# One hybrid encoder trunk: the order of a projection's outputs, weights and products

## The chip, the cores and the metric

The kernel runs on one core of a Trainium2 chip. The metric is the device time of one execution in microseconds; three runs of the kernel before took 2345.83, 2346.84 and 2350.24 us, so its median is 2346.84. TensorE is called PE in the profile's rows, VectorE DVE, ScalarE ACT, GpSimd POOL, and SP is the engine whose queue issues most loads and stores.

## The reference

Two layers over 1024 time steps of width 1024, all in float32. What matters here are the two wide projections of each layer and what is done with each of their columns:

```python
for l in range(DEPTH):                       # 2 layers
    h = rmsnorm(x, norm1_w[l])
    q, k, v, g, z, xbc, dt_raw, lru_gate, lru_x = split_proj(h @ w_in[l])
    y_ret = retention(q, k, v, g)            # rotary on q and k
    y_ssd = ssd(z, xbc, dt_raw, ...)         # causal conv of width 4 and SiLU on xbc
    y_lru = rglru(lru_gate, lru_x, ...)      # causal conv of width 4 on lru_x, GeLU on lru_gate
    x = x + concatenate([y_ret, y_ssd, y_lru]) @ w_out[l]
    h = rmsnorm(x, norm2_w[l])
    u, v = causal_dwconv(h @ w_up[l])        # width 3, 2 x 2816 columns
    x = x + (gelu(u) * v) @ w_down[l]
return rmsnorm(x, final_norm_w)
```

## The kernel before

Activations lie with the 1024 channels on partitions, in 8 tiles of 128 x 512 for each half of the time (XA the first half, XB the second). A float32 product is made from a high and a low part of both operands: high x high, high x low, low x high (`PASSES`), so one block product over four channel tiles, called a product here, is 12 matmuls of 128x128 by 128x512 (`mm3`, `prod`). The parts are made by ScalarE (a copy that rounds, L205 and L236) and VectorE (the difference, L206 and L243); for weights GpSimd may take the difference by an accumulating DMA (L241).

A projection works through pairs of 128-column blocks: 12 pairs in an input projection, 22 in a feed-forward one. A pair is a 2 x 2 x 2 block problem (two column blocks, two halves of the channels, two halves of the time) done with seven products instead of eight, in the Strassen-Winograd way. `start` makes two of them from the first time half (operands `b11`, `b21`): the first result is u, copied from its bank by ScalarE (L834), and c11, their sum on VectorE (L837). `end` makes five, with operands `t2`, `t3`, `t1`, `b22`, `t4` of both time halves, and adds them on VectorE to the four results (L874 to L890). Their five weights come from `prep`: four additions or subtractions of raw weights on VectorE (L710), and five splits. The first pair uses eight plain products instead, four in `lead` and four in `follow`, because the operands of the second half don't exist yet.

`take` is what is done with a finished result: in the feed-forward projection a convolution (ScalarE L315, VectorE L318), the GeLU (L931), the product of the two columns (L933) and a store (L934); in the input projection a convolution with a gate (`xbc`, `lru`), a gate (`silu2`, `gelu2`) or the rotary (`rotate`: loads, and three VectorE operations L382 to L384).

`products` sets the order. Its `rest(0)` to `rest(3)` make the second half's operands: the norm's sum and its rows, then the blocks: `t1` and `b22` in `rest(2)`, `t2`, `t3` and `t4` in `rest(3)` (`blocks_b`, on VectorE with ScalarE). In between stand the products that need only the first half: `lead` of the first pair (p0) and `start` of the second and third (p1, p2). Then p0's `follow`, p1's `end`, p2's `end`, and from the fourth pair on `start` and `end` in turn. In the first layer's input projection (`raw`) the first half isn't normalised before its products; `scaled` multiplies the results by the rows, and p0's, p1's and p2's takes come after `rest(2)`. In the other three projections a first result is taken as soon as it is made.

The program's order is a priority: a planner at build time places each instruction on its engine's queue when its operands and a free buffer are there, the earliest in the program first, and each engine then works its queue in that order. Buffers that play a part: eight split weights (`wsplit`), three raw weights (`wraw`), eight tiles `t` (c11, u3, c22, a convolution's output, the rotary's tables), five tiles `c` (u), four banks each of `pp` and `ps`. `flip` gives two of three weight differences to GpSimd from the fourth pair on.

## Time and profile before

| what | value |
|---|---|
| median of three runs | 2346.84 us (2345.83 to 2350.24) |
| the profiled execution | 2346.2 us, span 2344.4 |
| TensorE busy | 2174.7 us (93%), 10494 matmuls |
| VectorE busy | 1924.6 us (82%) |
| ScalarE busy | 1288.4 us (55%) |
| GpSimd busy | 302.6 us (13%) |
| mean granted TensorE clock | 0.970 |

In order of time the first layer's input projection takes about 17 to 334, its mixers to 420, the output projection to 519, the feed-forward projection 519 to 962, the down projection to 1181; the second layer's input projection 1181 to 1474, mixers to 1566, output projection to 1662, feed-forward 1662 to 2106, down projection and final norm to the end. Times in the text are us on this axis, the profiled execution's span. Rows by stage give each engine's busy time in a stretch; rows in order of time give an instruction's start and length, and in brackets how long its engine stood idle before and what ended that. A line of a helper (L236, L243, L710, L300) stands for all its callers, so the tiles' names tell which one it is: `up` is a bank of a projection, `ws` a split weight, `wr` a raw one, `s` the weight sum S2, `bl` the low part of an operand block, `fc` a feed-forward convolution, `dtc` and `dtt` the time steps of the state-space mixer. Matmul records are missing now and then.

### The profile page before, as it was taken

The page shows a single profiled execution, that of the slowest core. Times are in us where ns is not written, and L with a number is a line of the kernel's source. Part 1 is how long each engine was busy: PE and PEld are TensorE (multiplying, and loading weights), DVE is VectorE, ACT ScalarE, POOL GpSimd, SP SyncE. Part 2 cuts the span into 40 slices and gives each one's busy share as a digit, 9 for nine tenths or more (in the row PEclk, how much of TensorE's full clock was granted, in tenths as well). Part 3 has the DMA queues.
Part 4 walks back from the last instruction along what each step waited for, and adds up shares of the span by engine and source line. Part 5 has one row for each costly group of instructions (what it writes and reads, how often), then busy time and mean ns, then how long its engine had stood idle before and what let it go on. Part 6 is the DMA issues. An engine that isn't in the chain of part 4 may idle for free.

```text
span 2344.4 us, 31562 instructions
## 1 busy us (share of the span) xinstructions
PE 2174.7 (93%) x10494; PEld 1758.3 (75%) x10494; DVE 1924.6 (82%) x3763; ACT 1288.4 (55%) x2370; POOL 302.6 (13%) x335
## 2 busy tenths in 40 slices
PE   6699988997999999999978989899989999999997
PEld 4477767885788888878866767777668888887787
DVE  7987858779877788999798877696797788789987
ACT  5357637554566556444445674674556665654443
POOL 0012213000222222000001131210002222210000
PEclk9799999999999999999988999999989999999999
DMA  4365687561666666854334638846437666677522
GB/s 173 108 149 134 150 248 233 167 209 48 149 150 148 145 153 152 285 193 137 108 128 123 152 79 235 266 150 208 137 93 164 144 148 148 147 197 254 178 83 73
DMA packets 176147, 371.94 MB, mean 159 GB/s; under 512 B 19440, under 2 KB 31856, under 8 KB 175984
## 3 DMA queue, kind: packets, MB, share of 16 engines
q1 hardware_dynamic: 135760, 297.55, 38.6%
q0 software_dynamic: 37440, 68.17, 17.1%
q10 hardware_dynamic: 2784, 4.20, 0.5%
q8 instruction: 83, 1.36, 0.3%
q14 instruction: 80, 0.66, 0.1%
HBM read 228.22 MB, written 69.27 MB: 127 GB/s over the span
## 4 chain that ended last, share of the span: by engine, by line
PE 65%; DVE 15%; DMA 8%; issue 7%; ACT 3%; SPq 1%; POOL 1%; DVEq 0%; POOLq 0%; ACTq 0%
PE up L300 43%; PE op L300 6%; PE dy L995 5%; PE dx L995 5%; PE dx L1071 2%; DMA ws<-wr 2%; DVE ws L243 2%; DVE bl L206 1%; DVE xb L318 1%; DMA cumb<-cumscr 1%; DMA tb<-in_rope_dram 1%; DMA g<-g1scr 1%; DMA g<-g0scr 1%; DVE g L710 1%; DMA wr<-in_w_ct_dram 1%
## 5 line engine op out<-in xcount | busy, mean ns | idle before, releaser
L300 PE MATMUL up<-bh,ws 128*128 128x512 f32 x3840 | 1228.2, 400 | 76.4 <-ACT ws L236 50.5
L300 PEld LDWEIGHTS up<-bh,ws 128*128 128x128 f32 x3840 | 735.6, 192 | 249.7 <-ACT ws L236 54.0
L300 PE MATMUL up<-bl,ws 128*128 128x512 f32 x1920 | 761.1, 398 | 11.8 <-DVE bl L206 11.7
L236 ACT ACTIVATE ws<-wr 128x512 fp32r<-128x512 f32 x568 | 348.7, 626 | 358.9 <-PE up L300 129.0
L300 PEld LDWEIGHTS up<-bl,ws 128*128 128x128 f32 x1920 | 369.2, 192 | 102.3 <-DVE bl L206 22.4
L241 POOL DMA_DIRECT2D ws<-wr x222 | 197.6, 905 | 1321.5 <-ACT ws L240 1046.0
L243 DVE TENSOR_TENSOR ws<-wr,ws 128x512 fp32r<-128x512 f32 x346 | 236.5, 688 | 61.0 <-ACT ws L236 54.9
L995 PE MATMUL dy<-ws,ws 128*128 128x512 f32 x792 | 192.2, 390 | 3.2 <-ACT ws L236 1.6
L995 PE MATMUL dx<-ws,ws 128*128 128x512 f32 x792 | 190.8, 390 | 2.1 <-ACT ws L236 1.2
L995 PEld LDWEIGHTS dy<-ws,ws 128*128 128x128 f32 x792 | 148.2, 188 | 36.4 <-DVE ws L243 3.3
L995 PEld LDWEIGHTS dx<-ws,ws 128*128 128x128 f32 x792 | 148.4, 188 | 34.1 <-ACT ws L236 2.1
L318 DVE SCALAR_TENSOR_TENSOR fc<-u,smalls,fc 128x512 f32<-128x512 f32 (+2 forms) x176 | 131.0, 748 | 50.6 <-ACT fc L315 49.6
L240 ACT ACTIVATE ws<-ws 128x512 fp32r<-128x512 f32 x260 | 159.8, 626 | 4.6
L300 PE MATMUL op<-yh,ws 128*128 128x512 f32 x512 | 160.5, 394 | 0.2 <-ACT yh L213 0.2
L318 DVE SCALAR_TENSOR_TENSOR fc<-c,smalls,fc 128x512 f32<-128x512 f32 (+2 forms) x176 | 131.2, 745 | 0.7 <-ACT fc L315 0.3
L315 ACT ACTIVATE fc<-c,smalls 128x512 f32<-128x512 f32 x88 | 71.2, 809 | 103.7 <-DVE c L837 101.7
L243 DVE TENSOR_TENSOR ws<-g,ws 128x512 fp32r<-128x512 f32 (+1 forms) x165 | 103.1, 649 | 13.7 <-ACT ws L236 13.5
L236 ACT ACTIVATE ws<-g 128x512 fp32r<-128x512 f32 (+1 forms) x165 | 92.1, 590 | 39.7 <-PE dy L995 13.8
L300 PEld LDWEIGHTS op<-yh,ws 128*128 128x128 f32 x512 | 95.4, 188 | 21.7 <-ACT yh L213 2.1
L300 PE MATMUL op<-yl,ws 128*128 128x512 f32 x256 | 100.3, 394 | 0.0
L710 DVE TENSOR_TENSOR wr<-wr,wr 128x512 f32<-128x512 f32 x64 | 44.9, 702 | 63.0 <-DMA wr<-in_w_up_dram 28.3
L236 ACT ACTIVATE ws<-s 128x512 fp32r<-128x512 f32 x64 | 40.4, 632 | 101.3 <-DVE s L710 92.4
(303 smaller groups left out, 2939.3 us busy)
## 6 DMA issues: line engine op xcount, KB each, us to landing
ws<-wr POOLq DMA_DIRECT2D x222, 256.0 KB, 4.3
wr<-in_w_up_dram SPq DMA_DIRECT2D x96, 512.0 KB, 4.3
wr<-in_w_dn_dram SPq DMA_DIRECT2D x66, 512.0 KB, 3.9
wr<-in_w_ct_dram SPq DMA_DIRECT2D x56, 512.0 KB, 4.7
wr<-in_w_o_dram SPq DMA_DIRECT2D x32, 512.0 KB, 5.1
g0scr<-fc SPq DMA_DIRECT2D x44, 256.0 KB, 3.3
g<-g0scr SPq DMA_DIRECT2D x44, 256.0 KB, 5.8
g1scr<-fc SPq DMA_DIRECT2D x44, 256.0 KB, 2.9
```

Source lines behind the costliest of these rows:

```text
L206: eng.tensor_tensor(lo, src, hi.bitcast(F32), op=ALU.subtract)
L236: act.activation(w[:, 0, :m], raw, AF.Copy)
L240: act.activation(w[:, 1, :m], w[:, 0, :m].bitcast(F32), AF.Copy, scale=-1.0)
L241: pool.dma_start(w[:, 1, :m].bitcast(F32), raw, accum_op=ALU.add)
L243: eng.tensor_tensor(w[:, 1, :m], raw, w[:, 0, :m].bitcast(F32), op=ALU.subtract)
L300: pe.matmul(dst, W(k, a), A(k, b), start=first and i == 0, stop=last and i == n - 1)
L315: act.activation(dst, body(x), AF.Identity, bias=bias, scale=taps(n))
L318: dve.scalar_tensor_tensor(dst[:, o:HT], x[:, HALO - j + o : HALO - j + HT], taps(n - j), dst[:, o:HT], op0=ALU.mult, op1=ALU.add)
L710: eng.tensor_tensor(o, a, b, op=op)
L995: pe.matmul(d[oc], w[:, a, P * oc : P * oc + P], t[:, b], start=not more and i == 0 and k == 0, stop=i == NP - 1 and k == 2, skip_group_ch ...
L1071: pe.matmul(X[oc][:, e], w[x][:, P * oc : P * oc + P], t[:, y, e], start=False, stop=i == NP - 1 and k == 2, skip_group_check=True)
```

## The change

Three things are changed, for all four projections.

- The order in `products`. p0's `lead` and the two `start`s no longer take their results. After `rest(2)` come `scaled`, p0's `follow` without its takes, the `prep` of p1, `rest(3)`, and only then the takes of p0, first half (`firsts`) and second half (`followed`). p1's `prep`, which stood at the head of its `end`, thus goes in front of `rest(3)`, and each later pair's first results are taken just before its `end`. The first layer's case and the others now have one order; `lead` and `ahead` are fixed at 1 and 2.
- The order in `end`. The product of `t1` comes first, into a bank z; ScalarE copies z into c22, and the product of `b22` is accumulated into the same bank after that (`more` leaves out the start flag). One addition of u with z stands for two, and c22 is completed with u3 from memory. The order of products is t1, t2, b22, t3, t4 instead of t2, t3, t1, b22, t4.
- The order of the splits in `prep`: w1, w2, w4, w3, w22 instead of w2, w3, w1, w4, w22.

```diff
@@ -291,13 +291,13 @@
             return x
         return get
 
-    def mm3(dst, W, A, ks, first=True, last=True):
+    def mm3(dst, W, A, ks, first=True, last=True, more=False):
 
         n = 3 * len(ks)
         i = 0
         for k in ks:
             for a, b in PASSES:
-                pe.matmul(dst, W(k, a), A(k, b), start=first and i == 0, stop=last and i == n - 1)
+                pe.matmul(dst, W(k, a), A(k, b), start=first and i == 0, stop=last and i == n - 1, skip_group_check=more)
                 i += 1
 
 
@@ -781,8 +781,8 @@
         sp.dma_start(r[:, : 2 * HT], src)
         return r[:, :HT], r[:, HT : 2 * HT]
 
-    def prod(d, w, B, name, first=True, last=True):
-        mm3(d, lambda k, a: w[:, a, P * k : P * k + P], lambda k, b: B[name, k][b], range(4), first, last)
+    def prod(d, w, B, name, first=True, last=True, more=False):
+        mm3(d, lambda k, a: w[:, a, P * k : P * k + P], lambda k, b: B[name, k][b], range(4), first and not more, last, more)
 
     class Pair:
 
@@ -790,7 +790,7 @@
         def __init__(self, src, B, take):
             self.src, self.B, self.take, self.ready, self.w, self.q = src, B, take, None, None, None
 
-        def lead(self, raw):
+        def lead(self):
 
             B = self.B
             self.v = []
@@ -808,8 +808,6 @@
                 c = halo(t_tile, "c11")
                 dve.tensor_add(body(c), body(u), d2)
                 self.v.append((c, u))
-                if not raw:
-                    self.take(m, 0, c, u)
 
         def follow(self):
 
@@ -820,14 +818,14 @@
                 prod(d, w1, self.B, "t1", last=False)
                 prod(d, w2, self.B, "b22", first=False)
                 dve.tensor_add(body(u), body(u), d)
+
+        def followed(self):
+            for m, (_, u) in enumerate(self.v):
                 self.take(m, 1, u)
 
-        def start(self, reload=False, raw=False):
-            if self.ready:
-                w11, w12 = self.ready
-            else:
-                q = up_raw(self.src[0])
-                w11, w12 = part_of(q[0]), part_of(q[1])
+        def start(self, reload=False):
+            q = up_raw(self.src[0])
+            w11, w12 = part_of(q[0]), part_of(q[1])
             d1, d2 = p_bank("up"), s_bank("up")
             prod(d1, w11, self.B, "b11")
             self.u = halo(c_tile, "u")
@@ -837,15 +835,17 @@
             dve.tensor_add(body(c11), body(self.u), d2)
             self.q = None if reload else q
             self.v = [(c11, self.u)]
-            if not (reload and raw):
-                self.scaled()
 
         def scaled(self):
 
-            for m, (c, u) in enumerate(self.v):
-                if "raw" in self.B:
+            if "raw" in self.B:
+                for c, u in self.v:
                     dve.tensor_tensor(body(c), body(c), self.B["raw"], op=ALU.mult)
                     dve.tensor_tensor(body(u), body(u), self.B["raw"], op=ALU.mult)
+
+        def firsts(self):
+
+            for m, (c, u) in enumerate(self.v):
                 self.take(m, 0, c, u)
 
         def prep(self):
@@ -856,11 +856,10 @@
             s3 = a11
             s2 = tp.tile([P, HT], F32, tag="xl", name=nm("s2"), bufs=2)
             sub(dve, s2, a22, s3)
-            w2, w3 = part_of(s2), part_of(s3)
             sub(dve, a21, a21, a22, ALU.add)
-            w1 = part_of(a21)
+            w1, w2 = part_of(a21), part_of(s2)
             sub(dve, a12, a12, s2)
-            w4, w22 = part_of(a12), part_of(a22)
+            w4, w3, w22 = part_of(a12), part_of(s3), part_of(a22)
             self.w = w1, w2, w3, w4, w22
 
         def end(self):
@@ -869,21 +868,21 @@
                 self.prep()
             w1, w2, w3, w4, w22 = self.w
             u = body(U)
-            d = p_bank("up")
+            U3, C22 = halo(t_tile, "u3"), halo(t_tile, "c22")
+            u3, c22 = body(U3), body(C22)
+
+            z = p_bank("up")
+            prod(z, w1, B, "t1")
+            act.activation(c22, z, AF.Copy)
+            d = s_bank("up")
             prod(d, w2, B, "t2")
             dve.tensor_add(u, u, d)
+            prod(z, w4, B, "b22", more=True)
             d = s_bank("up")
             prod(d, w3, B, "t3")
-            U3, C22 = halo(t_tile, "u3"), halo(t_tile, "c22")
-            u3 = body(U3)
             dve.tensor_add(u3, u, d)
-            d = p_bank("up")
-            prod(d, w1, B, "t1")
-            dve.tensor_add(u, u, d)
-            dve.tensor_add(body(C22), u3, d)
-            d = s_bank("up")
-            prod(d, w4, B, "b22")
-            dve.tensor_add(u, u, d)
+            dve.tensor_add(u, u, z)
+            dve.tensor_add(c22, c22, u3)
             self.take(0, 1, U)
             d = p_bank("up")
             prod(d, w22, B, "t4")
@@ -891,30 +890,29 @@
             self.take(1, 0, U3, C22)
             self.take(1, 1, C22)
 
-
-    def products(pairs, rest, later, lead, ahead, raw=False):
-
-        n = lead + ahead
-        for j, p in enumerate(pairs[:n]):
-            if j < lead:
-                p.lead(raw)
-            else:
-                p.start(True, raw)
-            if j < n - 1:
-                rest(j)
-        rest(2)
-        for j, p in enumerate(pairs):
-            by_dma[0] = j >= n
-            if j >= n:
+    def products(pairs, rest, later, ahead=2):
+
+        p = pairs[0]
+        p.lead()
+        rest(0)
+        for j in range(1, ahead + 1):
+            pairs[j].start(True)
+            rest(j)
+        p.scaled()
+        p.follow()
+        pairs[1].prep()
+        rest(3)
+        p.firsts()
+        p.followed()
+        for f in later.get(0, ()):
+            f()
+        for j, p in enumerate(pairs[1:], 1):
+            by_dma[0] = j > ahead
+            if j > ahead:
                 p.start()
-            elif raw:
-                p.scaled()
-            if j == 1:
-                rest(3)
-            if j < lead:
-                p.follow()
-            else:
-                p.end()
+            p.scaled()
+            p.firsts()
+            p.end()
             for f in later.get(j, ()):
                 f()
         by_dma[0] = False
@@ -1233,7 +1231,7 @@
             rest = lead(B, XA, XB, first[0])
             pairs[0].ready = ready
         later = {0: [] if l else [setup], 1: [dt_a, dt_b], 3: [dt_c]}
-        products(pairs, rest, later, *((1, 2) if l else (1, 2)), not l)
+        products(pairs, rest, later)
         after = mixers(l, dts, skip(l))
         XA = out_proj(l, 0, y_split(l, 0, after), src)
         SB = y_split(l, 1, last_dma[0])
@@ -1250,7 +1248,7 @@
         XB = out_proj(l, 1, SB, src, hook)
         sB = squares(lambda k: XB[k], f=d_tile)
         spill(xs1, XB, 1)
-        products([ffn_pair(l, j, B) for j in range(NF)], rest_of(B, XA, XB, sB, w2), {}, *((1, 2) if l else (1, 2)))
+        products([ffn_pair(l, j, B) for j in range(NF)], rest_of(B, XA, XB, sB, w2), {})
         XA, XB, last, others = ffn_down(l, None)
         if l + 1 < DEPTH:
             B, st = {}, {}
```

## Rows read from the trace of the kernel before

**Rows 1.** Stages: us; busy PE, PEld, DVE, ACT, POOL; clock; DMA share; GB/s.

```profile
26.00:110.00 84.00, 57.44 (x213) 37.34 (x214) 80.60 (x176) 26.38 (x49) 0.00 (x0) 0.81 0.30 97
...
519.00:592.00 73.00, 58.44 (x231) 42.57 (x230) 64.60 (x121) 34.90 (x55) 0.00 (x0) 0.90 0.18 56
592.00:962.00 370.00, 370.00 (x1630) 306.28 (x1629) 298.08 (x498) 222.84 (x362) 75.94 (x88) 1.00 0.65 157
...
1181.00:1262.00 81.00, 59.11 (x246) 44.68 (x245) 74.36 (x136) 36.42 (x61) 0.86 (x1) 0.83 0.39 127
```

**Rows 2.** Waits in total: us, times, the longest; TensorE.

```profile
PE up L300 <- ACT ws L236: 50.5, 8, 17.1
```

**Rows 3.** Order of time, TensorE, 1221 to 1241: start, us, engine, line, operation, tiles [idle before].

```profile
1240.40 0.80 PE L300 MATMUL up<-bh,ws 128*128 128x512 f32 x1 [17.09 <-ACT ws L236]
```

**Rows 4.** Order of time, VectorE, 1236 to 1241.

```profile
1237.20 0.68 DVE L206 TENSOR_TENSOR bl<-xd,bh 128x512 fp32r<-128x512 f32 x1
1237.80 0.68 DVE L710 TENSOR_TENSOR wr<-wr,wr 128x512 f32<-128x512 f32 x1
...
1240.81 0.68 DVE L206 TENSOR_TENSOR bl<-xd,bh 128x512 fp32r<-128x512 f32 x1
```

**Rows 5.** Order of time, TensorE, 580 to 589.

```profile
587.94 0.79 PE L300 MATMUL up<-bh,ws 128*128 128x512 f32 x1 [5.42 <-ACT ws L236]
```

**Rows 6.** Order of time, VectorE, 582 to 588.

```profile
583.16 0.68 DVE L710 TENSOR_TENSOR wr<-wr,wr 128x512 f32<-128x512 f32 x1
583.76 2.73 DVE L318 SCALAR_TENSOR_TENSOR fc<-u,smalls,fc 128x512 f32<-128x512 f32 x4
...
586.48 0.68 DVE L710 TENSOR_TENSOR s<-wr,wr 128x512 f32<-128x512 f32 x1
```

**Rows 7.** Order of time, TensorE, 98 to 112.

```profile
109.28 0.60 PE L418 MATMUL dtt<-mats,dtc 16*128 16x16 f32 x4 [10.02 <-DVE dtc L413]
```

**Rows 8.** Order of time, VectorE, 111 to 113.

```profile
111.35 0.68 DVE L710 TENSOR_TENSOR wr<-wr,wr 128x512 f32<-128x512 f32 x1
```

**Rows 9.** Groups of VectorE, 1201.7 to 1209.2, then 1218.8 to 1240.3: count, busy, mean ns.

```profile
L318 DVE SCALAR_TENSOR_TENSOR xb<-c,smalls,xb 128x511 f32<-128x511 f32 (+2 forms) x3 | 2.2, 748 | 0.0
...
L382 DVE TENSOR_TENSOR u<-u,tb 128x512 f32<-128x512 f32 x2 | 1.4, 680 | 0.0
```

**Rows 10.** Order of time, TensorE, 1256 to 1266.

```profile
1256.71 0.40 PE L403 MATMUL dt<-bh,wds 128*16 128x512 f32 x1
...
1260.43 0.40 PE L300 MATMUL up<-bh,ws 128*128 128x512 f32 x1
...
1265.67 0.40 PE L403 MATMUL dt<-bh,wds 128*16 128x512 f32 x1
```

**Rows 11.** Order of time, load queue, 532 to 596.

```profile
575.19 1.55 SPq L781 DMA_DIRECT2D wr<-in_w_up_dram  x2
...
595.07 2.64 SPq L781 DMA_DIRECT2D wr<-in_w_up_dram  x2
```

**Rows 12.** Groups of the whole run.

```profile
L882 DVE TENSOR_TENSOR u<-u,up 128x512 f32<-128x512 f32 x64 | 43.7, 683 | 19.9 <-PE up L300 19.3
...
L834 ACT ACTIVATE u<-up 128x512 f32<-128x512 f32 x64 | 37.5, 586 | 19.7 <-PE up L300 19.7
```

**Rows 13.** Order of time within one pair: ScalarE, then VectorE.

```profile
684.08 0.57 ACT L834 ACTIVATE u<-up 128x512 f32<-128x512 f32 x1
...
688.28 0.82 ACT L315 ACTIVATE fc<-c,smalls 128x512 f32<-128x512 f32 x1 [3.11 <-DVE c L837]
...
687.57 0.68 DVE L837 TENSOR_TENSOR c<-u,up 128x512 f32<-128x512 f32 x1
...
692.25 0.74 DVE L318 SCALAR_TENSOR_TENSOR fc<-c,smalls,fc 128x510 f32<-128x510 f32 x1
...
697.26 0.69 DVE L886 TENSOR_TENSOR u<-u,up 128x512 f32<-128x512 f32 x1 [0.67 <-PE up L300]
```

**Rows 14.** Waits in total, ScalarE on VectorE.

```profile
ACT fc L315 <- DVE c L837: 101.7, 37, 4.1
```


## The prediction

> **What bounds the kernel now.** I read the busy time by stage first, then who waits for whom on TensorE, then the order of time around its longest stalls.
>
> By stage [rows 1], TensorE is busy for all 370 us of the middle of the first feed-forward projection: 1630 recorded matmuls, 370 / 1630 = 0.227 us each, so a product of 12 takes 2.72 us and a pair of 84 takes 19.1 us. VectorE is at 298 of 370 there. Nothing taken off VectorE or ScalarE can shorten that stretch. The starts of the four projections are different: in 26 to 110, 519 to 592 and 1181 to 1262 VectorE works 81 of 84, 65 of 73 and 74 of 81 us, TensorE 57 to 59, and its granted clock averages 0.81 to 0.90; the second feed-forward start, 1662 to 1735, repeats the first. These 311 us are bound by VectorE, which makes the second half's operands, the weight sums and the finished outputs in one queue.
>
> Among TensorE's waits [rows 2] one for a split weight lasted 17.1 us. In time it lies at 1223 to 1240, in the second layer's input projection [rows 3]. All that p1 (the second pair) then needs is weights, but its first subtraction `wr<-wr,wr` starts only at 1237.80, among the last block splits [rows 4]. In the feed-forward starts the 5.42 us at 582.5 to 587.9 [rows 5] wait for p2 (the third pair): its subtractions stand at 583.16 and 586.48, with four convolution operations of p1's outputs between [rows 6]. In the first input projection the 10.02 us end at 109.28 [rows 7], with p2's subtractions at 111.35 [rows 8].
>
> **The change, part by part.** VectorE's operations start 0.60 us apart when it is saturated [rows 4]; I count with that, and 0.66 for a convolution's.
>
> (a) *First results behind the blocks.* In the second layer's input projection 8 operations of outputs ran among the first blocks (1201.7 to 1209.2: three convolution, three rotary, two gate, of which the first kind is shown), 8 x 0.62 = 5.0 us, and 6 rotary ones, 3.6 us, among the last [rows 9]. All 14 go behind the last block.
>
> (b) *p1's weights ahead of them.* Three of its four subtractions already stood before the last block; one subtraction and five splits, 6 x 0.60 = 3.6 us, are new in front. The last block then ends at 1241.5 - 5.0 - 3.6 + 3.6 = 1236.5 (1241.5 is 1240.81 + 0.68 in [rows 4]), and p1's last product 2.7 us later, at 1239, where now it ends at 1256.7 [rows 10]. The stall of 17 us goes.
>
> What is late next is p2: its weight sums stand behind everything put off. 14 output operations (8.6 us), p1's 5 additions (3.0), p1's three own convolutions with gates (3 x (3 x 0.66 + 0.6), 7.7), then three subtractions (1.8): 1236.5 + 21.1 = 1257.6, and about 0.9 for the split. So p2 begins at 1258.5, against 1260.4 now [rows 10]: 1.9 us. The work is conserved; what is gained beside it is what TensorE can do in the wait: 16 time-step matmuls that now stand behind p2's start (16 x 0.23 = 3.7 [rows 10]) and the two first products of p3 (24 x 0.227 = 5.4). Together 11.0; I take 9, because the two products need weights through the same load queue as the rotary tables. Bounds: 0 if VectorE's order keeps both out, 17.1 if p2's sums slip ahead of the outputs.
>
> In the feed-forward starts p1's weights are mostly made already. p2's start there is conserved less one addition (0.6). But its raw loads, now at 575.2, wait for p1's last two splits, and p3's come at 595 [rows 11]. With p1's splits ahead of the blocks both come before 575, and p3's two products (5.4) fit into the wait for p2: 6.0, of which I take 5, twice. Bounds for each: 3.0 us lost (five of p1's output operations, now after the subtraction, come before it because p1 ended sooner) to 8.4 gained (the 5.42 and 3 of slow restart). In the first input projection outputs stood behind two blocks' rounds already; the same sum gives 6.0, and I take 4, since `dtc` stays where it is in VectorE's queue. Bounds: 2 lost, 10.0 gained.
>
> More is issued past each queue: the loads of p1's weights go ahead of 24 rotary loads on the load queue, which shields them; the output stores come later, and nobody reads them in this stage. Tiles are the hidden cost: four first results are now held to the end of the blocks in a pool of eight, from which the rotation's three, and p1's two outputs, come too. A shortage delays outputs, not blocks.
>
> (c) *S1 T1 first, S4 B22 in its bank.* For 64 pairs VectorE loses one addition of six, the first on the bank of t1, 43.7 us in all; the other is kept, from memory instead of the bank. ScalarE gains a copy like the one of the first product, 37.5 us per 64 [rows 12]. In the middles both are hidden by TensorE's full queue [rows 1]: nothing. In the starts the addition is in the 0.6 above. The matmul count is unchanged. New is a wait: B22's product may not write the bank until ScalarE has copied it. Between stands t2's product, 2.72 us, against a copy of 0.59. The nearest row is the copy of a pair's first product: L886 begins at 697.26, released by its product, so the first product of that pair ended five products earlier, 697.2 - 13.6 = 683.6, and its copy began at 684.08 [rows 13]: 0.5 late, where 2.1 may be lost. I take nothing; the bounds are nothing and the second rival. If the cover goes, everything on TensorE behind that matmul waits, weight splits behind the copy on ScalarE too.
>
> Queue order, weighed: ScalarE's next convolution waited until 688.28, 3.11 us, for a VectorE sum [rows 13], and 37 such waits took 101.7 us, the longest 4.1 [rows 14]. The Trainium skill ("TensorE: Matmul & The Clock Gate", on engine queue depths) says that ScalarE takes its queue strictly in order, so that a copy behind such a wait waits too. By the row alone the sum keeps its zero; by that rule it would be the second rival's, and the trace agrees as far as order goes.
>
> **Sum.** 9 + 4 + 5 + 5 = 23 us off the profiled execution's 2346.2 (span 2344.4 and 1.8 around it) gives 2323.2; the median 2346.84 lies 0.64 above it, so 2324.
>
> **Rivals.** *The stalls only move* (0.18). VectorE's work ahead of p2 is conserved, and p3's weights don't arrive: four times 0.6 is left, 2344 to 2345. For it: VectorE is busy for 65 to 81 us of those stretches. Against it: TensorE had no filler because raw tiles came late, and these come sooner.
>
> *The copy holds up TensorE in the middles* (0.17, the slower one). If ScalarE's order puts the copy behind p's first GeLU, it waits for the sum L837, a convolution and two VectorE operations, the last of which starts at 692.25 and ends at 692.99, 6.6 us after the second product's end at 686.4; with GeLU (0.62) and copy (0.59) the bank is read at 7.8, where t1 and t2 allow 5.4. Each such pair costs 2.4 us; it decides from 1 pair in 5 on (10 of the 42 feed-forward pairs eat the 23 us). At 2 in 5, 17 x 2.4 = 41: 2365. For it: the waits of [rows 14] come once in nearly every pair. Against it: without the GeLU in front the copy ends 1.2 + 0.68 + 0.81 + 0.59 = 3.3 us after the second product, 2.1 us in time.
>
> *p2's sums slip ahead* (0.15). If held tiles stall the outputs, VectorE turns to p2 at once: 17.1 + 10.0 + 2 x 8.4 = 44 off, 2302.
>
> **Chances.** The forecast has 0.50, with its own range 2311 to 2337. From 2300 to 2358 about 8 in 10 is held: below is the tail of the last rival, above most of the slower one. A measurement can tell 0.2%, 4.7 us, from no change: faster is the forecast, the last rival and a quarter of the first (0.68), the same the rest of the first (0.15), slower the second rival (0.17).
>
> **What would show it.** Right: no TensorE wait of 17 us in the second input projection, with p1's first subtraction before its last round of blocks; p1's last product there ends near 1239 on this axis; a wait for p2's weights follows; p3's first products stand ahead of p2's others; the middles stay at 19.1 us a pair. Wrong: matmuls in the middles that wait for ScalarE's copy; p2's start unmoved with nothing new ahead of it; outputs in the stretch of the blocks as before.

## The result: 0.55% slower, and the profile after

The changed kernel took 2360.93 us (median of four runs, 2356.99 to 2363.38) against 2348.32 us of the kernel before on the same chip: a ratio of 1.0055, interval 1.0039 to 1.0071. The forecast, 23 us faster, was wrong in sign. The profiled execution took 2356.99 us with a span of 2355.2.

The part of the page with busy time:

```profile
PE 2180.1 (93%) x10494; PEld 1753.2 (74%) x10494; DVE 1896.9 (81%) x3699; ACT 1314.6 (56%) x2434; POOL 304.9 (13%) x335
```

VectorE has 64 operations less and ScalarE 64 more, as the change says. By stage, in the same columns and stretches, moved with each stage's start, as [rows 1]:

```profile
26.00:110.00 84.00, 63.41 (x234) 41.95 (x234) 79.53 (x173) 30.54 (x57) 1.00 (x1) 0.82 0.31 94
525.00:598.00 73.00, 62.07 (x249) 44.99 (x247) 65.47 (x122) 35.60 (x57) 0.00 (x0) 0.93 0.18 59
598.00:973.00 375.00, 371.63 (x1635) 306.87 (x1636) 284.95 (x476) 230.95 (x383) 75.94 (x88) 1.00 0.66 158
1188.00:1269.00 81.00, 68.09 (x283) 49.32 (x282) 79.37 (x145) 37.30 (x64) 0.86 (x1) 0.92 0.41 128
```

The starts look as forecast: 18 to 37 matmuls more in each, VectorE at least about as full as before (79.5 of 84, 65.5 of 73 and 79.4 of 81 us). New is the third line. The middle of the first feed-forward projection, where TensorE had no idle time before, now has 375.00 - 371.63 = 3.4 us of it. TensorE's waits in total (us, times, the longest) show what is new:

```profile
PE up L300 <- ACT ws L236: 43.4, 10, 8.1
PE up L300 <- ACT c L876: 16.7, 12, 3.2
...
PE dtt L418 <- DVE dtc L413: 7.5, 1, 7.5
PE dtt L418 <- DVE dtc L415: 6.9, 2, 6.6
```

Waits for split weights fell from 50.5 us [rows 2]; L876, the new copy of T1's bank, is a new group of 16.7; and the second layer's time-step transposes, which did not wait before, wait 6.6.

Order of time, TensorE, second layer's input projection, whose start is now at 1188.2 (1181.0 before):

```profile
1246.60 0.80 PE L300 MATMUL up<-bh,ws 128*128 128x512 f32 x1 [3.18 <-ACT ws L236]
...
1267.34 0.60 PE L418 MATMUL dtt<-mats,dtc 16*128 16x16 f32 x4 [6.57 <-DVE dtc L415]
```

The 17.09 us of [rows 3] are gone. The first line is already the first product of p2. VectorE's order in the same stretch shows why it is so early:

```profile
1221.26 0.70 DVE L710 TENSOR_TENSOR wr<-wr,s 128x512 f32<-128x512 f32 x1
...
1236.53 0.69 DVE L382 TENSOR_TENSOR c<-c,tb 128x512 f32<-128x512 f32 x1
...
1241.95 0.69 DVE L206 TENSOR_TENSOR bl<-xd,bh 128x512 fp32r<-128x512 f32 x1
...
1243.82 0.69 DVE L710 TENSOR_TENSOR wr<-wr,wr 128x512 f32<-128x512 f32 x1
...
1251.40 0.75 DVE L318 SCALAR_TENSOR_TENSOR xb<-c,smalls,xb 128x511 f32<-128x511 f32 x1
```

p1's last subtraction now stands at 1221.26, the last block's low part at 1241.95, and three operations behind it, at 1243.82, p2's first subtraction; most of the outputs that the forecast put in between (a convolution at 1251.40) come after. Not all 14 went behind the last block, either: six rotary operations (L382 to L384, the first at 1236.53) still run among the last low parts, as many as the forecast counted there before [rows 9]. The last block's low part still ends 54.4 us after the stage's start where it ended at 60.5, a little sooner than the forecast's 55.5.

The second group of waits, in one pair of the first feed-forward (p5): ScalarE's two lines, then TensorE's two:

```profile
658.15 0.81 ACT L315 ACTIVATE fc<-c,smalls 128x512 f32<-128x512 f32 x1 [5.21 <-DVE c L835]
658.88 0.58 ACT L876 ACTIVATE c<-up 128x512 f32<-128x512 f32 x1
...
657.25 0.39 PE L300 MATMUL up<-bh,ws 128*128 128x512 f32 x1
659.50 0.50 PE L300 MATMUL up<-bh,ws 128*128 128x512 f32 x1 [1.87 <-ACT c L876]
```

T2's last matmul begins at 657.25 and ends at 657.64, so T1's product ended 2.72 us before that, at 654.9. Its copy begins only at 658.88, 4.0 us later, because it stands behind a convolution that waited 5.21 us for a VectorE sum. T2's product covers 2.7 of 4.0 + 0.6; the rest, 1.9, is TensorE's idle time before B22. VectorE shows why that sum, L835, was late:

```profile
654.24 0.69 DVE L710 TENSOR_TENSOR wr<-wr,wr 128x512 f32<-128x512 f32 x1 [3.04 <-DMA wr<-in_w_up_dram]
...
657.44 0.68 DVE L835 TENSOR_TENSOR c<-u,up 128x512 f32<-128x512 f32 x1
```

It stands behind a subtraction that waited 3.04 us for its raw weights, and four more operations. So one late load is handed on through two queues before it reaches TensorE.

### The profile page after: what moved, and what is told of

Read it like the earlier page. It is cut to its first block, busy times and chain, and to the rows that moved or that the text cites. A ratio compares the mean times of both kernels' runs of the same rounds, so it can differ in the third digit from the quotient of the medians.

```text
span 2355.2 us, 31426 instructions
## 1 busy us (share of the span) xinstructions
PE 2180.1 (93%) x10494; PEld 1753.2 (74%) x10494; DVE 1896.9 (81%) x3699; ACT 1314.6 (56%) x2434; POOL 304.9 (13%) x335
## 5 line engine op out<-in xcount | busy, mean ns | idle before, releaser
L318 DVE SCALAR_TENSOR_TENSOR fc<-u,smalls,fc 128x512 f32<-128x512 f32 (+2 forms) x176 | 130.4, 749 | 12.3 <-ACT fc L315 11.8
L883 DVE TENSOR_TENSOR u<-u,up 128x512 f32<-128x512 f32 x64 | 43.9, 686 | 84.9 <-PE up L300 84.9
```

Of the source, the lines that this page charges most:

```text
L318: dve.scalar_tensor_tensor(dst[:, o:HT], x[:, HALO - j + o : HALO - j + HT], taps(n - j), dst[:, o:HT], op0=ALU.mult, op1=ALU.add)
L883: dve.tensor_add(u3, u, d)
```

## The experiments

All ratios are to the kernel before on the same chip, with 95% intervals. The stage lengths are read from one trace each: from a projection's first matmul to the next one's (the first from the span's start, the last to its end). For an input projection this takes in the mixers and the output projection, for a feed-forward one its down projection.

| kernel | ratio | input 1 | feed-forward 1 | input 2 | feed-forward 2 |
|---|---|---|---|---|---|
| before | 1 | 518.7 | 662.3 | 481.2 | 682.2 |
| changed | 1.0055 | 525.4 | 662.8 | 485.4 | 681.6 |
| e_order: (a), (b) alone | 1.0012 | 517.8 | 659.2 | 486.3 | 676.7 |
| e_end: (c) alone | 1.0156 | 523.4 | 668.9 | 498.7 | 686.4 |
| e_late: B22 behind T3 | 0.9962 | 519.7 | 659.1 | 481.0 | 677.5 |
| e_bank: B22's own bank | 1.0007 | 523.9 | 663.5 | 472.6 | 683.8 |
| e_split: before, split order | 1.0207 | 532.7 | 667.4 | 501.1 | 687.4 |
| e_endlate: (c) alone, B22 behind T3 | 1.0107 | 521.1 | 663.7 | 492.8 | 684.9 |
| e_hold: output projection held | 1.0062 | 526.2 | 663.3 | 490.1 | 682.8 |
| b_hold: before, held | 1.0008 | 518.0 | 661.4 | 479.6 | 678.9 |
| e_no_a | 1.0123 | 528.2 | 661.3 | 494.4 | 681.5 |
| e_no_b | 1.0091 | 522.7 | 663.0 | 490.3 | 683.8 |
| e_latesum | 1.0051 | 528.1 | 663.8 | 480.9 | 680.1 |
| e_last | 1.0005 | 519.3 | 658.2 | 490.1 | 676.8 |
| e_dvecopy | 1.0178 | 530.0 | 667.5 | 489.7 | 689.1 |
| e_ffn | 0.9982 | 517.7 | 660.4 | 479.1 | 677.6 |
| e_combo | 0.9948 | 513.0 | 659.5 | 474.3 | 678.5 |

How far a length can be read: the first input stage has the same code in before, e_ffn and e_combo and took 513.0 to 518.7. A difference of less than 6 us in one input stage says nothing by itself; the feed-forward stages with the same code (e_order, e_ffn, e_combo) agree within 1.8.

**The parts one by one.** e_order keeps the changed order of outputs and weights and takes the pair of before (`end` and the order of splits in `prep`); e_end is the reverse.

> The changed order of outputs and weights (parts a and b) with the pair of before (part c undone). Copy theory: the loss sits in the copy of the first bank, for which TensorE waited 16.7 us; without the copy that goes, and the mixers' stretch too if it is the pair's new times that shifted it: 2361 - 17 = 2344, or about 2338 with half of the mixers' 11.6 us. Layout theory: the mixers and output projections (+7.4 and +4.2 us, code untouched) lose because the order of outputs gave the planner other due times: they stay long, and only a few us come off, 2354 to 2361. Conservation theory (start gains are given back at the third pair's weights whatever the pair does): the four starts stay within 3 us of before's lengths, and the time is that of before, 2345 to 2349.

> The order of outputs and weights of before with the changed pair (part c alone). Copy theory: the 12 or so waits of TensorE for the copy come back at about 17 us: 2347 + 17 = 2364. Layout theory: the mixers run as before, and the waits are partly absorbed by stalls that follow: 2347 to 2354. If the 17.1 us stall of the second input projection is still there and nothing else moved, the difference to the kernel before is the price of the pair by itself.

Measured: 1.0012 (1.0001 to 1.0023) and 1.0156 (1.0140 to 1.0172). (a) and (b) by themselves are worth nothing, (c) by itself costs 36 us, more than any theory gave it; with (a) and (b) it costs 10. In e_order the long stall is gone too (2.59 us at 1235.13 in its place), and a wait late in the same stage, ahead of the last pair's five products, is longer than before. e_order's two lines, then that wait in the kernel before:

```profile
1235.13 0.79 PE L300 MATMUL up<-bh,ws 128*128 128x512 f32 x1 [2.59 <-ACT ws L236]
1457.74 0.79 PE L300 MATMUL up<-bh,ws 128*128 128x512 f32 x1 [8.32 <-ACT ws L236]
```

```profile
1464.84 0.79 PE L300 MATMUL up<-bh,ws 128*128 128x512 f32 x1 [4.77 <-ACT ws L236]
```

Counted from the stage's start, e_order was 18.5 us ahead of before at the 240th product matmul of that projection, 12.8 at the 260th, 2.9 at the projection's end, and 5.1 behind at the next projection's first matmul. In the feed-forward stages it kept 3.1 and 5.5.

**The copy's cover.** e_late moves one line; e_bank does without the copy.

```diff
             dve.tensor_add(u, u, d)
-            prod(z, w4, B, "b22", more=True)
             d = s_bank("up")
             prod(d, w3, B, "t3")
             dve.tensor_add(u3, u, d)
+            prod(z, w4, B, "b22", more=True)
```

> The changed kernel with B22's product behind T3's in the pair, so that two products (5.4 us) stand between T1 and the next write of its bank, where one (2.7 us) stood. Copy theory: TensorE's wait for the copy (16.7 us, longest 3.2) falls under 3 us and the time by about 14: 2361 - 14 = 2347. Layout theory: the mixers' stretches keep their +7.4 and +4.2 us; at most 5 us off, 2356 to 2361.

```diff
-            act.activation(c22, z, AF.Copy)
...
-            prod(z, w4, B, "b22", more=True)
+            z2 = p_bank("up")
+            prod(z2, w4, B, "b22")
...
-            dve.tensor_add(c22, c22, u3)
+            dve.tensor_add(c22, u3, z)
+            dve.tensor_add(u, u, z2)
```

> The changed kernel with B22 in a bank of its own: no copy on ScalarE (37.5 us less there), one VectorE addition more a pair (43.7 us per 64), the same order of products otherwise. Copy theory: no matmul waits for ScalarE's copy, 16.7 us go and the addition is hidden in the middles: about 2344 to 2347, up to 3 us more where the starts are bound by VectorE. Layout theory: 2356 to 2361, since the mixers keep their loss. A new wait that could show: a bank that is read later, so that the next product finds none free.

e_late: 0.9962 (0.9949 to 0.9976), 0.93% or 22 us under the changed kernel, more than the copy theory asked. e_bank: 1.0007 (0.9997 to 1.0016), 11 us under it. In e_late the two middles have lost most of their idle time (3.4 us in the first of the changed kernel, 371.00 - 369.75 = 1.25 here):

```profile
593.00:964.00 371.00, 369.75 (x1632) 305.78 (x1631) 288.71 (x478) 228.15 (x380) 75.96 (x88) 1.00 0.66 161
...
1733.00:2104.00 371.00, 370.05 (x1631) 305.93 (x1632) 288.68 (x478) 227.20 (x380) 75.86 (x88) 1.00 0.66 160
```

and none of the waits for L876 stands there. But they did not fall under 3 us in all, as the theory wanted:

```profile
PE up L300 <- ACT c L876: 11.0, 6, 4.3
```

All six stand in the input projections, together as long as the changed kernel's eight there (11.5 us of its 16.7). Of the 7.8 us won in the two feed-forward stages 4.6 are won by the projections' ends, and the copy's cover accounts for these: from the 240th product matmul to the projection's end the changed kernel loses 4.0 and 3.0 us against before, e_late 1.5 and 1.3, and e_order and e_bank, which have no such copy, nothing. The other 3.2 and the 10 us in the input stages came with the moved line without any such wait getting shorter there. (The two traces are of executions 18 us apart, so 4 of the 22 stand in no stage.)

**Is it the order of sums and splits?** (c) also changed `prep`. e_split is the kernel before with this alone; e_endlate is e_end with e_late's line moved.

```diff
-            w2, w3 = part_of(s2), part_of(s3)
             sub(dve, a21, a21, a22, ALU.add)
-            w1 = part_of(a21)
+            w1, w2 = part_of(a21), part_of(s2)
             sub(dve, a12, a12, s2)
-            w4, w22 = part_of(a12), part_of(a22)
+            w4, w3, w22 = part_of(a12), part_of(s3), part_of(a22)
```

> The kernel before with only the order of a pair's sums and splits of the changed one (w1, w2, w4, w3, w22, all three subtractions of the first two weights ahead); products and outputs as before. T2 is still multiplied first, so its weight now stands one subtraction and one split later. Copy theory (part c alone cost 35 us by waits for the copy): nothing here, 2340 to 2348. Split theory (part c alone cost 35 us because the first product's weight comes later where VectorE is the bound): 10 to 30 us of those 35 are here, 2354 to 2374, with longer waits for split weights in the four starts. Layout theory: the mixers shift by up to 7 us either way.

> The order of outputs of before, with the changed pair, B22's product behind T3's (part c alone, mended). Copy theory: the 35 us of the changed pair alone (2379 against 2344) go, except a few: 2344 to 2350. Split theory: only the 12 us of waits for the copy and their slow restarts go, 2360 to 2367.

e_split: 1.0207 (1.0194 to 1.0220), 48 us from an order of instructions. T2 still comes first in it, so its weight is later than the first product's in either pair, and the 48 us are not the price of this order inside (c), where T1 comes first. Its waits for split weights grew, also for those whose low part GpSimd makes by DMA; the wait ahead of the last pair's products in the second input projection is 11.53 us (4.77 before):

```profile
PE up L300 <- ACT ws L236: 64.5, 9, 18.8
...
PE up L300 <- DMA ws<-s: 12.2, 4, 5.5
...
1492.97 0.80 PE L300 MATMUL up<-bh,ws 128*128 128x512 f32 x1 [11.53 <-ACT ws L236]
```

e_endlate: 1.0107 (1.0094 to 1.0120), 2368 us, near the split theory's 2360 to 2367. The moved line gives back 11 of the 36 us of (c) alone, but not by the way that theory gave: the waits for the copy are 12.3 us in e_end and 10.9 in e_endlate, all in the input projections. So at most some 12 of the 36 us are such waits; of the rest the order of sums and splits is the one part tested.

**Does the output projection get in the mixers' way?** In the changed kernel its first matmul stands 8.0 us earlier among the last mixer chunks than before (406.55 against 414.59), and the next projection starts later. e_hold and b_hold tie its matmuls to the last chunk's last transpose.

```diff
-            mm3(d, wk(w), lambda k, b: S[k][b], YORD)
+            with tc.issue_after(held[0].ins):
+                mm3(d, wk(w), lambda k, b: S[k][b], YORD)
```

> The changed kernel with the output projection's matmuls held behind the last transpose of the last mixer chunk in TensorE's queue. Layout theory (output projection matmuls planned among the last chunks hold the mixers up): the 6.8 us lost by the start of the first feed-forward and the 4.2 us of the second layer come back, 2361 - 11 = 2350. Copy theory: the mixers' loss comes from copies that are late in the input projection; nothing comes back, and the mixers have less to fill their waits with: 2361 to 2368.

> The kernel before with the same hold, as the control of e_hold. Before already begins its output projection later among the chunks; if the hold costs filler, it shows here: 2344 to 2351. If it gains 5 us here too, e_hold's gain says nothing of the change.

1.0062 (1.0045 to 1.0079) and 1.0008 (0.9999 to 1.0018): nothing comes back. The layout theory falls in this form.

**(a) and (b) one at a time, in the changed kernel.** e_no_a has `products`, `lead`, `start`, `follow` and `scaled` of before, with `p.prep()` put ahead of `rest(3)`; e_no_b has the two lines changed over.

```diff
-        pairs[1].prep()
         rest(3)
+        pairs[1].prep()
```

> The changed kernel with part (a) alone undone: first results among the blocks as before, the second pair's weights ahead of the last blocks, the changed pair. If part (b) alone ended the 17 us stall: no TensorE wait over 8 us in the second input projection, and 2361 to 2366 in all (the feed-forward starts lose their 4.7 us each, part of what remains). If the stall needs (a) too, it comes back at 10 us or more: 2366 to 2372, towards the 2379 of the changed pair alone.

> The changed kernel with part (b) alone undone: the second pair's sums and splits behind the last blocks, ahead of the outputs put off. By the forecast's steps 3.6 us of VectorE come behind the last block in place of ahead of it, and p1 waits for its weights: a wait of about 4 us in the second input projection, 5.0 of the 17 us stall's way stays won: 2361 to 2368. If the second pair's weights don't matter once the outputs are behind them: 2358 to 2362.

1.0123 (1.0104 to 1.0143) and 1.0091 (1.0075 to 1.0107). In e_no_a no wait in the first 80 us of that stage is over 3.4 us: (b) alone ends the stall. It gains nothing by that: at the 240th product matmul e_no_a is level with before, and its 2371 us lie outside the 2361 to 2366 expected for this case. In e_no_b 9.4 us of it are left, more than the 4 expected:

```profile
1231.12 1.22 PE L300 MATMUL up<-bh,ws 128*128 128x512 f32 x2 [9.36 <-DVE ws L243]
```

In the feed-forward starts e_no_b gains 4.4 us each on before by the 240th matmul, e_no_a 2.1 and 1.3. Both have (c), which alone loses 5.1 and 4.4 there (e_end); against that either part by itself gives more than half of what the two give together.

The four kernels with the one-product cover also show where the late copies of the feed-forward middles come from. In the changed kernel and e_no_b, which put the outputs off, the copies in p4 and p5 of each feed-forward begin 3.0 to 4.0 us after their product, and TensorE waits; all others from p3 on begin at most 1.3 us after it. In e_end and e_no_a, which don't put them off, none begins more than 1.2 us after it, and TensorE never waits for one there. Waits of a convolution for a VectorE sum are as many and as long without (a), in e_end:

```profile
ACT fc L315 <- DVE c L837: 101.7, 40, 3.7
```

The subtraction of raw weights that waited 3.04 us in p5 waited 1.29 in e_no_a. So it takes (a) and (c) together: with (a) the VectorE sum of p4 and p5 comes late, and (c) makes TensorE wait for a copy behind it. Why the raw weights come later with (a) no run shows.

**Three tries for a better version of the pair.** e_latesum is e_late with W1's sum made second and split at once; e_last has B22 behind T4, with its weight split last; e_dvecopy is the changed kernel with the copy on VectorE.

```diff
+            sub(dve, a21, a21, a22, ALU.add)
+            w1 = part_of(a21)
             s2 = tp.tile([P, HT], F32, tag="xl", name=nm("s2"), bufs=2)
             sub(dve, s2, a22, s3)
-            sub(dve, a21, a21, a22, ALU.add)
-            w1, w2 = part_of(a21), part_of(s2)
+            w2 = part_of(s2)
```

> The mended kernel (B22's product behind T3's) with W1's sum made second of the three and split at once, as T1 comes first in a pair. Split theory (the first product of a pair waits for its weight where VectorE is the bound): the first split is free one subtraction sooner; p2's wait of 5.9 us in each feed-forward start falls by 0.6 to 1.3 and the waits for split weights (42.7 us) by 3 to 8; 2333 - 5 = 2328. If another weight of the same pair is then late instead: 2331 to 2336.

```diff
-            prod(z, w4, B, "b22", more=True)
...
-            dve.tensor_add(u, u, z)
             dve.tensor_add(c22, c22, u3)
-            self.take(0, 1, U)
             d = p_bank("up")
             prod(d, w22, B, "t4")
             dve.tensor_add(u3, u3, d)
             self.take(1, 0, U3, C22)
+            prod(z, w4, B, "b22", more=True)
+            dve.tensor_add(u, u, z)
+            self.take(0, 1, U)
```

> The mended kernel with B22's product moved on, behind T4's, as the last of the pair (its weight split last too, the second output's results taken before the first's second half). Copy theory: the 11.0 us that TensorE still waits for the copy in the input projections (longest 4.3) fall to under 2, and 2333 becomes 2322 to 2328. If these waits only stand where TensorE would have waited anyway: 2331 to 2338.

```diff
-            act.activation(c22, z, AF.Copy)
+            dve.tensor_copy(c22, z)
```

> The changed kernel with T1's bank copied by VectorE instead of ScalarE, B22's product still behind T2's. If the copy is late because ScalarE, taking its queue in order, holds it behind a convolution that waits: VectorE's queue has no such waits in the middles, no matmul waits for the copy in the feed-forwards (both about 659 and 678 us, as with the mended pair), and 3 to 8 us are lost in the starts, where VectorE gets 64 copies of some 0.6 us: 2340 to 2350. If one product is too short for any copy: waits of 0.5 to 3 us for it in the feed-forwards stay, 2357 to 2368.

All three missed. e_latesum: 1.0051 (1.0037 to 1.0065). The wait of 5.9 us fell to 4.1 in both feed-forward starts, more than expected, and yet 21 us were lost against e_late; its waits for the copy rose to 18.3 us (e_late 11.0), and two of them stand in the feed-forward middles again, with two products as cover:

```profile
664.72 0.79 PE L300 MATMUL up<-bh,ws 128*128 128x512 f32 x1 [4.10 <-ACT c L877]
```

Around this one the stage falls back 6.8 us against e_late. e_last: 1.0005 (0.9995 to 1.0016); its waits for the copy are 9.2 us, hardly less, with three products between. ScalarE before the last of them:

```profile
1453.89 0.63 ACT L343 ACTIVATE gt<-c 128x512 f32<-128x512 f32 x1 [13.55 <-DVE c L835]
1454.43 0.58 ACT L876 ACTIVATE c<-up 128x512 f32<-128x512 f32 x1
```

A gate's activation waited 13.55 us for the VectorE sum L835, and the copy behind it; three products are 8.2 us.

e_dvecopy: 1.0178 (1.0158 to 1.0198): on VectorE the copy is late more often still, 26 times for 39.9 us. VectorE in one of them, then TensorE:

```profile
2014.52 0.69 DVE L710 TENSOR_TENSOR wr<-wr,wr 128x512 f32<-128x512 f32 x1 [3.19 <-DMA ws<-wr]
...
2016.51 0.68 DVE L876 COPY c<-up 128x512 f32<-128x512 f32 x1
...
2017.34 0.47 PE L300 MATMUL up<-bh,ws 128*128 128x512 f32 x1 [1.80 <-DVE c L876]
```

The copy stands behind a subtraction that waited 3.19 us, and three more operations. It is the same event as on ScalarE with another head of the queue, so ScalarE was not the cause; a copy queued behind an operation that waits was.

**Where does a gain stay?** e_ffn has `products` and `Pair` of e_order for the feed-forwards alone; e_combo also has those of e_bank for the second input projection.

```diff
-        products([ffn_pair(l, j, B) for j in range(NF)], rest_of(B, XA, XB, sB, w2), {}, *((1, 2) if l else (1, 2)))
+        productsF([ffn_pair(l, j, B) for j in range(NF)], rest_of(B, XA, XB, sB, w2), {})
...
-        products(pairs, rest, later, *((1, 2) if l else (1, 2)), not l)
+        if l:
+            productsB(pairs, rest, later)
+        else:
+            products(pairs, rest, later, 1, 2, True)
```

> Order (a) and (b) in the two feed-forward projections alone, with the pair of before everywhere; input projections in the order of before. If a stage's gain is its own: 518.7 and 481.2 us from one projection's start to the next as before, 659.2 and 676.7 as with the new order: 8.6 us off the profiled span, 2344 - 8.6 = 2335, ratio 0.9963. If what the feed-forwards gain is given back in the stages behind them: 2341 to 2346.

> As e_ffn, and the second layer's input projection with the new order and the pair that has a bank of its own for B22 (it took 472.6 us there against 481.2 before, where the changed pair took 485.4). If a stage's length is its own: another 8.6 us off, 2327, ratio 0.9927. If the 8.6 us hung on what came before that stage: the second layer's input projection and mixers take 481 to 486 us again, 2335 to 2340.

e_ffn: 0.9982 (0.9973 to 0.9992); its trace shows the feed-forward gains (1.9 and 4.6 us), but the time falls by 4.2 us, half of what was expected. e_combo: 0.9948 (0.9931 to 0.9964), 12 us, with 474.3 us in the second input stage, 6.9 under before. The first gain is half of what the stages said, the second, 8 us on top of e_ffn, nearly all. e_combo has the lowest ratio here, ahead of the kernel before and the changed one; its interval meets e_late's. Its waits for split weights:

```profile
PE up L300 <- ACT ws L236: 34.6, 8, 7.8
```

## Why the prediction was wrong, step by step

**The stall, (a) and (b) in the second input projection.** Right that it goes and that a wait for p2's weights follows. Right too that p1's subtractions come ahead of the last blocks. Its other numbers were off. p1's last product ends 67 us after the stage's start (before 76, forecast 58), because in TensorE's order its B22 now stands behind p2's first product. p2 begins at 58.4 us instead of the forecast's 77.5 (1258.5 - 1181): the mechanism of the third rival, p2's sums ahead of the outputs. But its price didn't follow. The put-off outputs and the time steps have to be made all the same, a wait of 6.57 us for `dtc` is new, and at the 240th product matmul the stage was 20.1 us ahead of before, but most of that is the time steps and their wait, which before had behind it by then; from the 260th on it was 5.8 ahead (9 forecast), at the projection's end level, and at the next projection's start 4.2 behind. It takes no copy for this: e_order, without (c), falls from 12.8 ahead to 2.9 by the projection's end. That looks like the first rival's point, work conserved, carried past the stretch that I summed, though no run tests which work takes the gain back. I ended the sum at p2's start and took what was won there as kept; the stage goes on for 400 us.

**The feed-forward starts.** Forecast -5 each; at the 240th matmul each was 4.7 us ahead, counted from its start. Right in size, not in its way. I had p2's start where it was and p3's first two products in the wait. The trace has the wait as long as before, with the same 204 product matmuls ahead of it, only sooner:

```profile
589.36 0.79 PE L300 MATMUL up<-bh,ws 128*128 128x512 f32 x1 [5.90 <-ACT ws L236]
```

It answers to [rows 5], 63.9 us after the stage's start where it was 69.3: VectorE got to p2's first subtraction 5.0 us earlier, and p3's products stayed behind p2's start.

**The first input projection.** Forecast -4; the stage took 6.8 more, all of it behind the projection, which ended 0.6 us sooner. Its wait of 10.02 [rows 7] became two:

```profile
98.65 0.80 PE L300 MATMUL up<-bh,ws 128*128 128x512 f32 x1 [7.09 <-ACT ws L236]
117.32 0.61 PE L418 MATMUL dtt<-mats,dtc 16*128 16x16 f32 x4 [7.51 <-DVE dtc L413]
```

**(c), taken as nothing.** "In the middles both are hidden ... nothing", and of the new wait: "I take nothing; the bounds are nothing and the second rival." The row it rested on was the copy of a pair's first product, 0.5 us late [rows 13]. Measured late by 4.0 in the pair shown above. This is the second rival's mechanism, a copy behind a ScalarE operation that waits for the sum, in fewer pairs: 4 of 42 feed-forward pairs (the rival took 17) wait 0.9 to 1.9 us each, and the two stages lose 4.0 and 3.0 us behind their starts, which is nearly all that the starts had won. The kind of wait stood in the prediction as a warning: 37 waits of a ScalarE convolution for a VectorE sum [rows 14], now

```profile
ACT fc L315 <- DVE c L835: 102.2, 36, 5.2
```

The Trainium skill ("TensorE: Matmul & The Clock Gate", on engine queue depths) says that ScalarE and VectorE take their queues strictly in order, and the trace agrees on both engines, by 5.21 us ahead of the copy on ScalarE and 3.19 on VectorE. Counting these waits would not have given the term: e_end has 40 of them and no late copy in a feed-forward. [rows 13] held where nothing was put off, as in e_end and e_no_a. What the forecast missed is that its own part (a) makes that sum late in p4 and p5; it priced (c) on a trace without (a).

**Behind the projections.** The prediction has no term for the mixers and the output projection, whose code is unchanged. From a projection's last product matmul to the next projection's first one these took 176.6 us in both layers before and 184.0 and 180.8 in the changed kernel: 7.4 and 4.2 us, about what the two input stages lost.

**The account: the steps that failed.** From the forecast's -23 us to the measured +13 are 36. e_order has (a) and (b) without (c): it measured +3 where 23 were to be gained, so 26 of the 36 stand in these two parts. By stage its trace gives -0.9, -3.1, +5.1 and -5.5 for the forecast's -4, -5, -9 and -5: the second input projection, where the sum ended at p2's start, is the term that failed most, by 14 us (2.9 ahead at the projection's end, 8.0 lost behind it), and the feed-forward starts came out about right. (This trace is 4.1 us under e_order's median, so its stages add up to -4.4.) The other 10 are (c) beside the two, forecast at nothing; some 7 us of feed-forward middles are its late copies. e_late is 22 us under the changed kernel, more than those 10, so the moved line does more than undo the price of (c). The chances of the prediction have a slip too: its own terms for "faster" add up to 0.695, not 0.68.

**Open.** Why the input stages of the changed kernel are 4.4 to 5.7 us longer than e_late's, when their waits for the copy are as long. The difference is spread over waits of up to 2 us in the mixers, and lies at the limit of what one trace can tell. Open too is why the stretch behind the second input projection is longer in most kernels that change that projection: 176.6 us before and 175.2 in e_ffn, but 184.6 in e_order, 185.7 in e_bank and 185.1 in e_combo (178.6 in e_late); e_hold shows only that the output projection's early matmuls are not it. Nor did any run show why the order of three subtractions and five splits moves the input stages by up to 20 us (e_split), or why an order that shortens the wait it was made for (e_latesum) lengthens others; only that these orders don't add up.

## What to carry to other kernels

Before an operation that frees a buffer is put on an engine's queue, look at what stands in front of it there: its delay can be a wait of that queue's head, not its own duration, and the cover must be as long as that or the dependency must go. Price each part on the kernel that has the other parts in it: here the late copies of the feed-forwards came only with (a) and (c) together. A stall of 17.1 us that is removed can give nothing by the end of its stage; follow the sum to there, not to the end of the stall. Test the parts singly and in pairs: here one part cost 36 us alone and 10 beside the others, and one line moved made the whole 0.38% faster instead of 0.55% slower.

## What the hardware showed that I had not expected

How long a copy of 0.58 us can wait. In the feed-forward middles two products (5.4 us) ended every wait for it in e_late, and left 4.10 and 3.19 us in e_latesum. In the input projections one product left 11.5 us of waits, two 11.0, three 9.2: the activation in front of the copy there waited up to 13.55 us for VectorE, and no such cover is that long.
